# RWKV preparation of a hybrid encoder block: neighbour sums, norm sums, gate weights and one product taken from GpSimd or moved

## The chip, the cores and the metric

The kernel runs on one core of a Trainium2 chip. A core has a matrix engine (TensorE, "PE"; its weight loads are "PEld"), a vector engine (VectorE, "DVE"), a scalar engine for functions and copies (ScalarE, "ACT"), a general engine (GpSimd, "POOL") and an engine that issues transfers (SyncE, "SP"). Each works through its own queue in order; they wait for each other through semaphores. Data lies in SBUF (128 partitions) or, for the results of TensorE, in PSUM. The metric is the device time of one execution in microseconds (us), as the median of several runs.

## The reference, cut to what matters

One encoder layer on 1024 tokens of width 1024: a norm, one projection whose columns feed windowed attention, a bidirectional RWKV-7 branch and branch gates; then an output projection, a feed-forward part and a gated embedding. The preparation of the RWKV branch computes, for r, k and v (512 columns each):

```python
zr = proj[..., O_RWKV:O_GATE]
zr = zr + shift_mu[i] * (centred_shift(zr) - zr)      # 0.5 * (left neighbour + right neighbour)
...
w_raw = w0 + tanh(wl) @ w2                            # per direction, low rank 64
decay = exp(-exp(-softplus(-w_raw) - 0.5))
a = sigmoid(a0 + al @ a2)                             # per direction, low rank 64
kk = k * k_k
kk = kk / maximum(sqrt(sum(kk * kk, -1)), 1e-12)      # per head of 64
k_dir = k * (1.0 + (a - 1.0) * k_a)
...
bonus = sum(r * k_dir * r_k) * v                      # per head, both directions
...
gates = sigmoid(proj[..., O_GATE:].reshape(b, s, 2, D_MODEL))
```

The scan over the tokens then uses r, decay, k_dir, v, -kk and kk * a, and runs once forward and once backward.

## The kernel before

All matmuls with full precision are done as three: an operand is split into a rounded high part and a low part (the rest), and hi x hi, hi x lo and lo x hi are added in PSUM. `split` (L186) makes the two: a cast on ScalarE (L188) and a subtraction (L189) on VectorE or GpSimd, as the caller says. `load_w` (L194) loads a block of weights through a staging tile and splits it; its subtraction is on GpSimd unless `lo_eng` is given. Projection blocks give VectorE; the gates give none.

The stages follow each other: norm and q, k, v of the attention; the RWKV preparation (some 110 to 370 us of the profiled execution); attention; the chunked scan; the up projections, the output projection, the feed-forward part and the embedding. The program is written as a list of tiles and operations; a planner orders each engine's instructions at build time by its own costs and by the order of the program, except where the program pins them, and adds the waits. A tile with `bufs=n` has n buffers, and a new tile of that name waits until the oldest is free.

The preparation walks over four head pairs p (128 columns each). In order of the program, for one p:

- `keys` (L641): the k projection (48 matmuls of 512 columns, in two halves of the tokens), `shifted`, the squares of k * k_k (L644, ScalarE), their split for the norm sums.
- `normed_keys` (L649): the r projection by `proj_with`, which calls a hook after 36 of the 48 matmuls (`RH`): there the norm sums (`sums2`, L593 and L594: four matmuls with a matrix of ones) and a maximum with 1e-24 from PSUM (L655, VectorE). Behind the projection `shifted` for r, Ln and Exp (L658, L659, each with a table load on ScalarE) and the normed keys `kk` (L661).
- `direction(0)` (L667): the low-rank product for the decay (`lora`, four matmuls L569 and L571, Tanh from PSUM L573), scaled (L670) and summed along the chunks (L672); Exp of it both ways (`E`, `Ei`, L682 and L683); its last column kept (`Dt`, L684); -kk * E (L687, VectorE) and r * E (L688, GpSimd) into `ra`; the low-rank product for a; `kd` (L691, L692), `ta` (L693), the two halves of `bk` (L695, L696); r_k times kd (`rk`, L698, VectorE). `ra` and `bk` are stored by SP (L702, L703).
- the v projection with a hook after eight matmuls, which does the bonus sums of the pair before; `shifted` for v; the two low-rank products of the backward direction; `keys` of the next p; `direction(1)` (L700, L701 for rk); the bonus of this p begins; `normed_keys` of the next p.

`shifted` (L532) takes a projection from PSUM: ScalarE copies it once plainly into `zr`, which has a zero column on either side (L539), and once scaled by 1 - mu into `z` (L542). GpSimd adds the left and the right neighbour into `sm` (L544), and VectorE adds half of mu times it to `z` (L545). `zr` and `sm` have one buffer, `z` has four. The projections' PSUM tile `mm` has two banks, the others (`px`) six, the low-rank tile `th` two buffers.

The last pair has no next keys; gate projections (`gates`, L304) stand in for them. `fill0` (L618) takes a number of steps of them from `F0` at five points of the last pair. Each gate block has 24 matmuls, two weight loads of 256 KB, and a Tanh that goes out to HBM (L312, L313). What is left of them is done within the attention stage at the lowest priority.

Of the kernel before, what the change touches and what calls it, by code (L numbers as in the profile page):

```python
# [9 lines left out]
F32 = mybir.dt.float32  # L10
F32R = mybir.dt.float32r
AF = mybir.ActivationFunctionType
ALU = mybir.AluOpType
# [4 lines left out]
P = 128  # L18
T = 1024
DM = 1024  # L20
NT = T // P
KT = DM // P
C = 64
NCH = T // C
NP = 4
# [4 lines left out]
O_RWKV = 768  # L30
# [11 lines left out]
RH = 36  # L42
# [11 lines left out]
F0 = (28, 28, 28, 28, 40)  # L54
# [17 lines left out]
W_SCALE = -0.5 * float(np.exp(np.float64(-0.5)))  # L72
# [66 lines left out]
def block_kernel(ctx: ExitStack, tc: tile.TileContext, I: dict, out: bass.AP):  # L139
    nc = tc.nc  # L140
# [353 lines left out]
    def col(name, j):  # L494
        return pc[:, PC[name] + j:PC[name] + j + 1]


    with ExitStack() as s1:
# [15 lines left out]
        nc.vector.memset(wsc, W_SCALE)  # L514
        hka = A1.tile([P, 4], F32, name="hka")
# [16 lines left out]
        def shifted(c0, mi, pss=None, pin=False):  # L532
            pss = pss or proj(c0)
            zr = A1.tile([P, T + 2], F32, name="zr", bufs=1)
            nc.vector.memset(zr[:, 0:1], 0.0)
            nc.vector.memset(zr[:, T + 1:T + 2], 0.0)
            zc = z = A1.tile([P, T], F32, name="z", bufs=4)
            for h in range(2):
                a = nc.scalar.copy(zr[:, 1 + 512 * h:513 + 512 * h], pss[h])  # L539
                if pin and h == 0:  # L540
                    tc.keep_in_program_order(a)
                nc.scalar.activation(out=zc[:, 512 * h:512 * h + 512], in_=pss[h], func=AF.Copy, scale=omm[:, mi:mi + 1])  # L542
            sm = A1.tile([P, T], F32, name="sm", bufs=1)
            nc.gpsimd.tensor_tensor(out=sm, in0=zr[:, 0:T], in1=zr[:, 2:T + 2], op=ALU.add)  # L544
            a = nc.vector.scalar_tensor_tensor(out=z, in0=sm, scalar=hmu[:, mi:mi + 1], in1=zc, op0=ALU.mult, op1=ALU.add)  # L545
            if pin:
                tc.keep_in_program_order(a)
            return z
# [99 lines left out]

        def normed_keys(p, kz, sums):  # L649

            ri = nrm[:, 1]

            def norms():
                for hs, ps in next(sums):
                    nc.vector.tensor_scalar_max(ri[:, hs], ps, 1e-24)  # L655

            rz = shifted(O_RWKV + p * P, p, proj_with(O_RWKV + p * P, {RH: norms}))
            nc.scalar.activation(out=ri, in_=ri, func=AF.Ln)  # L658
            nc.scalar.activation(out=ri, in_=ri, func=AF.Exp, scale=-0.5)  # L659
            kk = A1.tile([P, T], F32, name="kk", bufs=1)  # L660
            nc.vector.scalar_tensor_tensor(out=kk, in0=kz, scalar=col("k_k", p), in1=ri, op0=ALU.mult, op1=ALU.mult)  # L661
            return kz, rz, kk

        def ch(x):
            return x.rearrange("p (c t) -> p c t", t=C)

        def direction(d, p, th, ta, kz, rz, kk, rk):  # L667

            th = th()
            nc.scalar.activation(out=th, in_=th, func=AF.Identity, scale=W_SCALE, bias=wsc)  # L670
            sl = slice(None) if d == 0 else slice(None, None, -1)
            nc.vector.tensor_tensor_scan(out=th[:, sl], data0=scan, data1=th[:, sl], initial=0.0, op0=ALU.mult, op1=ALU.add)  # L672
# [15 lines left out]
            nc.gpsimd.tensor_tensor(out=ra[:, :, 1, :], in0=ch(rz), in1=E2, op=ALU.mult)  # L688
            ta = ta()
# [7 lines left out]
            if d == 0:  # L697
                nc.vector.tensor_scalar_mul(rk, kd, col("r_k", p))  # L698
# [8 lines left out]
        for p in range(NP):  # L707
# [3 lines left out]
            def low_rank(d, i):  # L711
                th = lora(d, p, i, 8 * i + d * NP + p)
                fill0(p, 2 * d + i)
                return th
# [14 lines left out]
        fill0(NP - 1, 4)  # L729
# [1130 lines left out]
```

## Time and profile before

| what | us |
|---|---|
| median of 3 runs | 1809.24 |
| lowest and highest of them | 1803.22, 1815.18 |
| the profiled execution | 1803.17 |
| its span, first to last instruction | 1801.4 |
| TensorE busy | 1702.8 (95%) |
| VectorE, ScalarE, GpSimd busy | 1147.4 (64%), 882.0 (49%), 279.0 (15%) |

A row of the profile's groups or of its timeline gives line, engine, operation, the tile written and the tiles read, the shape, and times; in square brackets or at the end stands the idle time before the instruction and what ended it. In a group "x3 | 3.8, 1276 |" is the count, the busy time in us and the mean of one in ns. A list of waits gives the total in us, the number and the longest. Rows of stretches give the width and, for each engine, busy us and the number of instructions, then the granted TensorE clock (1 is full), the share of the DMA engines and GB/s. Matmuls are pipelined, so that their durations overlap: the distance of their starts counts.

### The profile page before, as it was taken

The page shows a single profiled execution, that of the slowest core. Times are in us where ns is not written, and L with a number is a line of the kernel's source. Part 1 is how long each engine was busy: PE and PEld are TensorE (multiplying, and loading weights), DVE is VectorE, ACT ScalarE, POOL GpSimd, SP SyncE. Part 2 cuts the span into 40 slices and gives each one's busy share as a digit, 9 for nine tenths or more (in the row PEclk, how much of TensorE's full clock was granted, in tenths as well). Part 3 has the DMA queues.
Part 4 walks back from the last instruction along what each step waited for, and adds up shares of the span by engine and source line. Part 5 has one row for each costly group of instructions (what it writes and reads, how often), then busy time and mean ns, then how long its engine had stood idle before and what let it go on. Part 6 is the DMA issues. An engine that isn't in the chain of part 4 may idle for free. (4 is left out here: it accounts for less than half of the span.)

```text
span 1801.4 us, 29643 instructions
## 1 busy us (share of the span) xinstructions
PE 1702.8 (95%) x11288; PEld 1367.5 (76%) x11288; DVE 1147.4 (64%) x1955; ACT 882.0 (49%) x1624; POOL 279.0 (15%) x241
## 2 busy tenths in 40 slices
PE   7999998899999898989889989999999999999998
PEld 7987675666677777867568867888888888888887
DVE  5667887345936556676564387767666877685432
ACT  5546775357754555456632255444444444554221
POOL 3343223331232121111232000000000000000000
PEclk9999999999999999999999999999999999999999
DMA  5353446574377474576565305454456983674111
GB/s 199 96 136 120 145 144 198 159 198 116 102 205 204 132 201 142 172 204 206 176 218 179 106 36 164 158 164 141 150 166 224 324 258 114 191 222 134 60 41 47
DMA packets 281998, 285.96 MB, mean 159 GB/s; under 512 B 49408, under 2 KB 195712, under 8 KB 281728
## 3 DMA queue, kind: packets, MB, share of 16 engines
q1 hardware_dynamic: 273600, 270.76, 48.9%
q0 software_dynamic: 7824, 12.59, 2.5%
q8 instruction: 89, 1.46, 0.3%
q10 hardware_dynamic: 432, 0.73, 0.1%
q14 instruction: 53, 0.43, 0.1%
HBM read 203.26 MB, written 80.74 MB: 158 GB/s over the span
## 5 line engine op out<-in xcount | busy, mean ns | idle before, releaser
L1742 PE MATMUL ff2ps<-th,sl 128*128 128x512 f32 x448 | 174.3, 389 | 0.0
L1742 PE MATMUL ff2ps<-tl,sh 128*128 128x512 f32 x448 | 174.3, 389 | 0.0
L1742 PE MATMUL ff2ps<-th,sh 128*128 128x512 f32 x448 | 173.9, 389 | 0.0
L189 POOL TENSOR_TENSOR wlo<-wst,whi 128x512 fp32r<-128x512 f32 x76 | 104.6, 1389 | 269.2 <-ACT whi L188 223.6
L176 POOL TENSOR_TENSOR rstd<-ms,neghalf 128x1 f32<-128x1 f32 x24 | 13.2, 552 | 791.3 <-DVE ms L174 791.3
L188 ACT CAST sh<-sst 128x512 fp32r<-128x512 f32 x109 | 67.7, 622 | 99.9 <-PE ff2ps L1742 51.3
L189 DVE TENSOR_TENSOR sl<-sst,sh 128x512 fp32r<-128x512 f32 x109 | 75.0, 688 | 47.5 <-ACT sh L188 47.3
L1742 PEld LDWEIGHTS ff2ps<-th,sh 128*128 128x128 f32 x448 | 84.0, 188 | 17.9 <-ACT th L188 0.3
L1742 PEld LDWEIGHTS ff2ps<-tl,sh 128*128 128x128 f32 x448 | 84.1, 188 | 17.6
L1742 PEld LDWEIGHTS ff2ps<-th,sl 128*128 128x128 f32 x448 | 84.1, 188 | 17.3
L188 ACT CAST whi<-wst 128x512 fp32r<-128x512 f32 x100 | 60.4, 617 | 60.8 <-DMA wst<-in_w_in_dram 22.9
L188 ACT CAST w1h<-w1st 128x512 fp32r<-128x512 f32 x48 | 28.4, 620 | 100.1 <-DMA w1st<-in_w_ff_dram 66.6
L189 DVE TENSOR_TENSOR w1l<-w1st,w1h 128x512 fp32r<-128x512 f32 x48 | 31.8, 687 | 54.5 <-ACT w1h L188 54.5
L209 PE MATMUL gps<-rm,bkp 128*128 128x256 f32 x256 | 62.4, 386 | 1.6 <-ACT tm L1105 0.9
L1078 DVE TENSOR_TENSOR gm<-gps,gmask 128x512 f32<-128x512 f32 x64 | 43.8, 688 | 29.6 <-PE gps L209 29.6
L219 PE MATMUL mm<-hh,wlo 128*128 128x512 f32 x144 | 58.4, 406 | 2.5 <-DVE wlo L189 2.5
L215 PE MATMUL gmm<-hh,whi 128*128 128x512 f32 x144 | 58.9, 409 | 1.6 <-ACT whi L188 1.4
L219 PE MATMUL gmm<-hh,wlo 128*128 128x512 f32 x144 | 59.3, 412 | 1.1 <-POOL wlo L189 1.1
L215 PE MATMUL mm<-hh,whi 128*128 128x512 f32 x144 | 58.6, 407 | 1.7 <-ACT whi L188 1.7
L217 PE MATMUL gmm<-hl,whi 128*128 128x512 f32 x144 | 58.7, 408 | 0.0
L217 PE MATMUL mm<-hl,whi 128*128 128x512 f32 x144 | 57.9, 402 | 0.0
L209 PEld LDWEIGHTS gps<-rm,bkp 128*128 128x128 f32 x256 | 47.2, 189 | 11.3 <-ACT tm L1105 2.1
(410 smaller groups left out, 4975.2 us busy)
## 6 DMA issues: line engine op xcount, KB each, us to landing
wst<-in_w_in_dram SPq DMA_DIRECT2D x92, 256.0 KB, 3.6
tst<-in_w_ff_dram SPq DMA_DIRECT2D x80, 256.0 KB, 3.9
w1st<-in_w_ff_dram SPq DMA_DIRECT2D x32, 512.0 KB, 5.4
hid_S<-h SPq DMA_DIRECT2D x64, 256.0 KB, 2.1
sst<-hid_S SPq DMA_DIRECT2D x64, 256.0 KB, 3.1
hid_A<-h SPq DMA_DIRECT2D x48, 256.0 KB, 2.0
sst<-hid_A SPq DMA_DIRECT2D x45, 256.0 KB, 3.5
ra_d<-ra SPq DMA_DIRECT2D x8, 1024.0 KB, 4.6
```

Of the source, the lines that this page charges most:

```text
L176: nc.gpsimd.tensor_tensor(out=r, in0=ms, in1=neghalf.broadcast_to([P, width]), op=ALU.pow)
L188: a = nc.scalar.copy(hi, src)
L189: b = (lo_eng or nc.vector).tensor_tensor(out=lo, in0=src, in1=hi.bitcast(F32), op=ALU.subtract)
L209: tc.keep_in_program_order(nc.tensor.matmul(*a, **kw))
L215: mm(ps, ah, bh, start=(i == 0), stop=False)
L217: mm(ps, ah, bl, start=False, stop=False)
L219: mm(ps, al, bh, start=False, stop=(i == n - 1))
L1078: nc.vector.tensor_tensor(out=gm[d][:, s % NB, 4 * h:4 * h + 4, :], in0=ps.rearrange("p j q t -> p (j q) t"), in1=gmask[:, d, :].unsqueeze ...
L1742: nc.tensor.matmul(banks[bs][i], x_[:, isl], y_, start=fresh and p + j == 0, stop=p == NPR - 1 and j == 2, skip_group_check=True)
```

## The change

- `shifted`: the copy into `zr` is scaled by half of mu; two additions on VectorE, of the left and then the right neighbour, go into `z`. `sm` and the GpSimd addition are gone; `zr` has two buffers.
- `normed_keys`: the decay's low-rank product of the forward direction, its scaling and its sum (`decays`) come ahead of the r projection, the product for a behind it, and the norm sums behind that, with no hook. The maximum becomes a Relu with a bias of -1e-24 on ScalarE, from PSUM, and Ln gets a bias of 1e-24.
- `direction`: r * E is on VectorE, the first `rk` on ScalarE; the low-rank tiles come from outside.
- the gates of the first seven blocks have their low parts made by VectorE; the filling steps of the last pair come at three points (56, 56, 40) rather than five (28, 28, 28, 28, 40).

```diff
-RH = 36
...
-F0 = (28, 28, 28, 28, 40)
+F0 = (56, 56, 40)
...
-    def gates(h, ms=range(2 * KT), mm=nc.tensor.matmul):
+    def gates(h, ms=range(2 * KT), mm=nc.tensor.matmul, lo_of=lambda m: nc.gpsimd):
...
-            hi, lo = load_w(PW, "w", w_in[:, :, c0:c0 + P], P, parts=2)
+            hi, lo = load_w(PW, "w", w_in[:, :, c0:c0 + P], P, parts=2, lo_eng=lo_of(m))
...
+        tiny = A1.tile([P, 2], F32, name="tiny")
+        nc.vector.memset(tiny[:, 0:1], -1e-24)
+        nc.vector.memset(tiny[:, 1:2], 1e-24)
...
-            zr = A1.tile([P, T + 2], F32, name="zr", bufs=1)
+            zr = A1.tile([P, T + 2], F32, name="zr", bufs=2)
...
-            zc = z = A1.tile([P, T], F32, name="z", bufs=4)
+            z = A1.tile([P, T], F32, name="z", bufs=4)
             for h in range(2):
-                a = nc.scalar.copy(zr[:, 1 + 512 * h:513 + 512 * h], pss[h])
...
-                nc.scalar.activation(out=zc[:, 512 * h:512 * h + 512], in_=pss[h], func=AF.Copy, scale=omm[:, mi:mi + 1])
-            sm = A1.tile([P, T], F32, name="sm", bufs=1)
-            nc.gpsimd.tensor_tensor(out=sm, in0=zr[:, 0:T], in1=zr[:, 2:T + 2], op=ALU.add)
-            a = nc.vector.scalar_tensor_tensor(out=z, in0=sm, scalar=hmu[:, mi:mi + 1], in1=zc, op0=ALU.mult, op1=ALU.add)
...
+                nc.scalar.activation(out=zr[:, 1 + 512 * h:513 + 512 * h], in_=pss[h], func=AF.Copy, scale=hmu[:, mi:mi + 1])
+                nc.scalar.activation(out=z[:, 512 * h:512 * h + 512], in_=pss[h], func=AF.Copy, scale=omm[:, mi:mi + 1])
+            for i in (0, 2):
+                nc.vector.tensor_tensor(out=z, in0=z, in1=zr[:, i:i + T], op=ALU.add)
             return z
...
-        gates0 = gates(0)
+        gates0 = gates(0, lo_of=lambda m: nc.vector if 25 * m < sum(F0) else nc.gpsimd)
...
+        def low_rank(p, d, i):
+            return lora(d, p, i, 8 * i + d * NP + p)
+
         def normed_keys(p, kz, sums):
 
             ri = nrm[:, 1]
-
-            def norms():
-                for hs, ps in next(sums):
-                    nc.vector.tensor_scalar_max(ri[:, hs], ps, 1e-24)
-
-            rz = shifted(O_RWKV + p * P, p, proj_with(O_RWKV + p * P, {RH: norms}))
-            nc.scalar.activation(out=ri, in_=ri, func=AF.Ln)
+            th = decays(0, low_rank(p, 0, 0))
+            rz = shifted(O_RWKV + p * P, p)
+            ta = low_rank(p, 0, 1)
+
+            for hs, ps in next(sums):
+                nc.scalar.activation(out=ri[:, hs], in_=ps, func=AF.Relu, bias=tiny[:, 0:1])
+            nc.scalar.activation(out=ri, in_=ri, func=AF.Ln, bias=tiny[:, 1:2])
             nc.scalar.activation(out=ri, in_=ri, func=AF.Exp, scale=-0.5)
...
-            return kz, rz, kk
+            return th, ta, kz, rz, kk
...
+        def decays(d, th):
+
+            nc.scalar.activation(out=th, in_=th, func=AF.Identity, scale=W_SCALE, bias=wsc)
+            sl = along(d)
+            nc.vector.tensor_tensor_scan(out=th[:, sl], data0=scan, data1=th[:, sl], initial=0.0, op0=ALU.mult, op1=ALU.add)
+            return th
+
         def direction(d, p, th, ta, kz, rz, kk, rk):
...
-            nc.gpsimd.tensor_tensor(out=ra[:, :, 1, :], in0=ch(rz), in1=E2, op=ALU.mult)
-            ta = ta()
+            nc.vector.tensor_tensor(out=ra[:, :, 1, :], in0=ch(rz), in1=E2, op=ALU.mult)
...
             if d == 0:
-                nc.vector.tensor_scalar_mul(rk, kd, col("r_k", p))
+                nc.scalar.activation(out=rk, in_=kd, func=AF.Copy, scale=col("r_k", p))
...
+            fill0(p, 0)
             rk = A1.tile([P, T], F32, name="rk", bufs=1)
-            direction(0, p, lambda: low_rank(0, 0), lambda: low_rank(0, 1), *ops, rk)
+            direction(0, p, *ops, rk)
             vz = shifted(O_RWKV + 1024 + p * P, 8 + p, proj_with(O_RWKV + 1024 + p * P, {VH: lambda: bonus and next(bonus)}))
-            lows_ = [low_rank(1, i) for i in range(2)]
+            th, ta = (low_rank(p, 1, i) for i in range(2))
+            fill0(p, 1)
             nxt = keys(p + 1) if p + 1 < NP else None
-            direction(1, p, lambda: lows_[0], lambda: lows_[1], *ops, rk)
+            direction(1, p, decays(1, th), ta, *ops[2:], rk)
...
-        fill0(NP - 1, 4)
+        fill0(NP - 1, 2)
```

More of the change, by code (lines that the diff above doesn't have):

```diff
@@ L530, in block_kernel, with shifted @@
         nc.sync.dma_start(scan, I["scan"])
[L532 removed]
+        def shifted(c0, mi, pss=None):
             pss = pss or proj(c0)
[L534 removed]
+            zr = A1.tile([P, T + 2], F32, name="zr", bufs=2)
             nc.vector.memset(zr[:, 0:1], 0.0)
             nc.vector.memset(zr[:, T + 1:T + 2], 0.0)
[L537 removed]
+            z = A1.tile([P, T], F32, name="z", bufs=4)
             for h in range(2):
[L539 to L547 removed]
+                nc.scalar.activation(out=zr[:, 1 + 512 * h:513 + 512 * h], in_=pss[h], func=AF.Copy, scale=hmu[:, mi:mi + 1])
+                nc.scalar.activation(out=z[:, 512 * h:512 * h + 512], in_=pss[h], func=AF.Copy, scale=omm[:, mi:mi + 1])
+            for i in (0, 2):
+                nc.vector.tensor_tensor(out=z, in0=z, in1=zr[:, i:i + T], op=ALU.add)
             return z
@@ L661, in normed_keys, with along @@
             nc.vector.scalar_tensor_tensor(out=kk, in0=kz, scalar=col("k_k", p), in1=ri, op0=ALU.mult, op1=ALU.mult)
-            return kz, rz, kk
+            return th, ta, kz, rz, kk
         def ch(x):
             return x.rearrange("p (c t) -> p c t", t=C)
+        def along(d):
+            return slice(None) if d == 0 else slice(None, None, -1)
+        def decays(d, th):
[3 more added lines that the diff above has]
+            return th
         def direction(d, p, th, ta, kz, rz, kk, rk):
[L669 to L672, printed above, removed]
+            sl = along(d)
             Lc = ch(th)
```

4 lines of the change are left out of this document (removed).

## The prediction

> **What bounds the kernel now.** I read the page first: one core, and TensorE all but full.
>
> ```profile
> span 1801.4 us, 29643 instructions
> PE 1702.8 (95%) x11288; PEld 1367.5 (76%) x11288; DVE 1147.4 (64%) x1955; ACT 882.0 (49%) x1624; POOL 279.0 (15%) x241
> ```
>
> The profiled execution took 1803.17 us, 1.8 more than its span. With PE at 95%, a change that leaves every matmul in place can pay only by the time in which PE waits, and by the slow matmuls after a wait. So the second view is the waits of PE inside the preparation and what follows it (110 to 400 us); the columns are the total, the number and the longest.
>
> ```profile
> PE px L593 <- ACT s L188: 11.1, 3, 4.6
> PE px L594 <- DVE s2l L189: 2.8, 1, 2.8
> PE mm L219 <- DVE wlo L189: 2.5, 2, 1.4
> ...
> PE mm L215 <- ACT whi L188: 1.7, 1, 1.7
> PE gmm L215 <- ACT whi L188: 1.4, 1, 1.4
> PE gmm L219 <- POOL wlo L189: 1.1, 2, 0.6
> ```
>
> These are 20.6 us. More than half is one place, met three times: the norm sums (L593), which stand inside the r projection after 36 of its 48 matmuls and want the hi part `s` of the squared keys. The first head pair has no such wait. The third view is PE in order of time. Each pair of rows is the first matmul after a wait and the first at full pace again; three pairs are norm sums, the fourth the bonus sums of the last pair.
>
> ```profile
> 186.25 0.80 PE L593 MATMUL px<-s,one_r 128*128 128x512 f32 x1 [4.04 <-ACT s L188]
> 189.60 0.40 PE L219 MATMUL mm<-hh,wlo 128*128 128x512 f32 x1
> ...
> 231.82 0.49 PE L593 MATMUL px<-s,one_r 128*128 128x512 f32 x1 [2.46 <-ACT s L188]
> 237.37 0.63 PE L569 MATMUL px<-lr,wlrh 128*128 128x512 f32 x2
> ...
> 280.10 0.80 PE L593 MATMUL px<-s,one_r 128*128 128x512 f32 x1 [4.57 <-ACT s L188]
> 285.17 0.39 PE L215 MATMUL mm<-hh,whi 128*128 128x512 f32 x1
> ...
> 353.95 0.79 PE L594 MATMUL px<-s2l,one_r 128*128 128x512 f32 x1 [2.77 <-DVE s2l L189]
> 360.08 0.43 PE L215 MATMUL gmm<-hh,whi 128*128 128x512 f32 x1
> ```
>
> Between 280.10 and 285.17 stand 11 matmuls, 0.46 us apart, where the pace elsewhere is 0.23: 5.07 - 11 x 0.23 = 2.5 us lost on top of the wait. By the same count the others lose 1.7 (7 matmuls), 2.1 (14, with a second wait of 0.23) and 2.9 (14). A norm wait thus costs 5.8, 4.8 and 7.1 us: **17.7 in all**.
>
> The Trainium skill ("TensorE: Matmul & The Clock Gate", Part 1) says that the clock halves after an idle window of about 3.4 us. By that rule the waits of 2.46 and 2.77 us would be followed by no slow stretch, and the sum below would be 2.1 lower; here both were, so the rows decide.
>
> Why is `s` late? The fourth view is the stretch before the wait at 231.82.
>
> ```profile
> 222.13 1.99 POOL L544 TENSOR_TENSOR sm<-zr 128x1024 f32<-128x1024 f32 x1 [0.93 <-POOL ra L688]
> 222.29 2.91 DVE L695 SCALAR_TENSOR_TENSOR bk<-th,Ei 128x1024 f32<-128x1024 f32 x1
> 228.66 1.27 DVE L545 SCALAR_TENSOR_TENSOR z<-sm,hmu,z 128x1024 f32<-128x1024 f32 x1
> 229.97 1.15 ACT L644 ACTIVATE nrm<-z,pc 128x1024 f32<-128x1024 f32 x1 [7.38 <-DVE z L545]
> ```
>
> POOL has the neighbour sum at 224.12, VectorE adds it only at 228.66, behind the backward direction's products, and ScalarE stands 7.38 us for it. VectorE is what is late, and it is slowed by POOL:
>
> ```profile
> 202.00 0.17 DVE L684 COPY Dt<-E 128x16 f32<-128x16 f32 x1
> 202.09 3.25 DVE L687 SCALAR_TENSOR_TENSOR ra<-kk,E 128x1024 f32<-128x1024 f32 x1
> ...
> 207.53 1.21 DVE L695 SCALAR_TENSOR_TENSOR bk<-th,Ei 128x1024 f32<-128x1024 f32 x1
> 208.67 2.38 DVE L698 TENSOR_SCALAR rk<-kd,pc 128x1024 f32<-128x1024 f32 x1
> ...
> 219.07 2.17 DVE L684 COPY Dt<-E 128x16 f32<-128x16 f32 x1
> 221.15 1.21 DVE L687 SCALAR_TENSOR_TENSOR ra<-kk,E 128x1024 f32<-128x1024 f32 x1
> ```
>
> ```profile
> 218.10 3.10 POOL L688 TENSOR_TENSOR ra<-z,E 128x1024 f32<-128x1024 f32 x1 [7.61 <-ACT E L682]
> ```
>
> ```profile
> 165.59 0.74 DVE L698 TENSOR_SCALAR rk<-kd,pc 128x1024 f32<-128x1024 f32 x1
> ```
>
> The same copy takes 0.17 alone and 2.17 beside POOL's 218.10 to 221.20; likewise 3.25 against 1.21, 2.38 against 0.74, 2.91 against 1.21. One cycle (one head pair) loses 2.00 + 2.04 + 1.64 + 1.70 = 7.4 us so.
>
> **The change part by part.** One cycle, from norm sums to norm sums, and the stretch after the last of them, with the busy time of PE, its weight loads, VectorE, ScalarE and POOL:
>
> ```profile
> 186.25:231.82 45.57, 43.11 (x176) 32.66 (x177) 40.21 (x44) 31.48 (x45) 11.31 (x5) 0.96 0.49 147
> ...
> 280.10:373.05 92.95, 82.25 (x321) 61.00 (x321) 45.82 (x38) 43.39 (x66) 39.85 (x29) 0.94 0.60 183
> ```
>
> PE's share without its wait and its slow stretch is 45.57 - 2.46 - 1.7 = 41.4; VectorE is busy 40.2, ScalarE 31.5. The prices:
>
> ```profile
> L672 DVE TENSOR_TENSOR_SCAN th<-scan,th 128x1024 f32<-128x1024 f32 x2 | 4.6, 2286 | 1.2 <-ACT th L670 1.2
> ...
> L655 DVE TENSOR_SCALAR nrm<-px 128x512 f32<-128x512 f32 x2 | 1.4, 691 | 0.5 <-PE px L594 0.5
> ```
>
> ```profile
> L573 ACT ACTIVATE th<-px,hb 128x512 f32<-128x512 f32 x8 | 4.9, 693 | 0.0
> ...
> L691 ACT ACTIVATE kd<-th,oka,hka 128x1024 f32<-128x1024 f32 x2 | 2.5, 1274 | 0.0
> ```
>
> *Neighbour sums as two additions, three times a cycle.* An addition of a tile with a copy of itself shifted by one element is not in the trace. From below 0.74 (the one-input form of that size), from above 3.25; I take 1.21, the two-input rows alone. So 2 x 1.21 - 1.27 (the row of 228.66) = +1.15 each, +3.4. POOL's part goes. *r by E on VectorE*: two of 1.21, +2.4. *Maximum to ScalarE as Relu*: -1.4 on VectorE; on ScalarE 2 x 0.69 as L573, which also reads PSUM with a bias. Bounds nothing (hidden in ScalarE's free time) and 1.27 (L691, twice the size); 0.69 because L573 has the same shape and form. *First rk to ScalarE*: -0.74, +1.27 as L691. *Scaled copies for plain ones*: six, each at no more than L573's 0.69; I count 0.1 more for each, +0.6. *Locks gone*: -7.4.
> VectorE: 40.2 + 3.4 + 2.4 - 1.4 - 0.7 - 7.4 = **36.5**; ScalarE 31.5 + 1.4 + 1.3 + 0.6 = **34.8**. Both lie under PE's 41.4, and PE becomes the bound of the cycle.
>
> *Norm sums moved behind the low-rank products.* They pass the last 12 matmuls of r (12 x 0.23 = 2.8) and two low-rank products:
>
> ```profile
> 147.06 0.73 PE L569 MATMUL px<-lr,wlrh 128*128 128x512 f32 x2
> ...
> 148.38 0.50 PE L215 MATMUL mm<-hh,whi 128*128 128x512 f32 x1
> ```
>
> 1.3 us for one product. PE asks for the sums 2.8 + 2.6 = 5.4 us later, and each of the three waits (4.04, 2.69, 4.57) is shorter than that. They would be gone if `s` came no earlier. Will it come later? At worst the moved first scan (2.3), the second addition (1.15) and one new r by E (1.21) all go ahead of it, 4.7; in that stretch the locks give back 2.00 + 1.70, so `s` is 1.0 late against a spare of 1.4, 2.7 and 0.8. At best the key's additions no longer wait for POOL and run 5 us sooner. The moved low-rank product issues no DMA; the weights two projections ahead are asked for where they were, on SP. Relu, Ln and Exp wait for the later sums on ScalarE, and behind them stand the copies that free the PSUM banks for v: that is the wait the change adds (a rival). The second low-rank tile has two buffers, and its Tanh can wait for the last bk.
> I take the 17.7 whole.
>
> *After the last norm sums* the gate projections fill PE. By the list of PE's waits they are 1.1 for POOL's wlo, 1.7 and 1.4 for ScalarE's whi, 2.5 for VectorE's wlo, and the 2.8 with 2.9 of slow matmuls: 12.4 in all.
>
> ```profile
> 308.03 0.69 ACT L573 ACTIVATE th<-px,hb 128x512 f32<-128x512 f32 x1 [3.01 <-DVE bk L695]
> 308.62 0.61 ACT L188 CAST whi<-wst 128x512 fp32r<-128x512 f32 x1
> ```
>
> ScalarE's cast for v's weights stood behind a Tanh that waited for VectorE's bk, so the 1.7, and the 2.5 with it, stem from VectorE's products of that stretch. With the locks gone I count both: -4.2, from nothing (POOL's gate parts held VectorE too, and seven of them now run on it) to that. The 2.8 comes from a scratch tile that the gates use too, the 1.4 from a weight load; I leave them.
> *Low parts of seven gates on VectorE*: 14 instructions of 0.68 instead of POOL's 1.47.
>
> ```profile
> L189 POOL TENSOR_TENSOR wlo<-wst,whi 128x512 fp32r<-128x512 f32 x36 | 52.5, 1470 | 89.5 <-ACT whi L188 89.5
> L189 DVE TENSOR_TENSOR wlo<-wst,whi 128x512 fp32r<-128x512 f32 x24 | 15.7, 683 | 9.5 <-ACT whi L188 9.5
> ```
>
> That is 9.5 us on an engine that was busy 46 of these 93; but in its queue they stand behind products of 1.21 each, and behind each stands SP's next weight load, which waits for its staging tile. From -2.5 (the 1.1 and the 1.4 go) to +39 (the slower rival below); I take +1.7, one more wait like the largest one here. The blocks of 56 gate steps put four to five weight loads ahead of the first direction's stores; the stores are read only in the next stage.
>
> **Sum:** 17.7 + 4.2 - 1.7 = 20.2 us less, 1803.2 to 1783.0 for the profiled execution. The median of the three runs shown is 1809.24, 6 above that execution (they lie from 1803.22 to 1815.18), so **1789.0**. Gates not done here are done in the attention stage; PE's work is only moved.
>
> **The rivals.** *All waits go*, the bonus wait too: 17.7 + 12.4, 1779. For it: POOL idle, VectorE 5 us a cycle below PE. Against: the 2.8 is not POOL's.
> *The wait moves*: ScalarE keeps its order, and v's first matmul waits for a PSUM bank behind Square, Relu and Ln. For it: ScalarE stood 7.38 us before Square with ready copies behind. Against: the Square no longer waits for POOL. Half of the 17.7 stays: 1797; all of it: 1806.
> *The change doesn't do what it says*: the long VectorE instructions are long for another reason than POOL. VectorE is then 43.9 a cycle, above PE's 41.4: three cycles of 2.5 are lost, and the 4.2 too: 20.2 - 11.7 = 8.5 less, 1801. Against: all four coincide with a POOL instruction. The Trainium skill ("SBUF — State Buffer", Who interferes with whom) says that POOL and VectorE share a pair of SBUF ports, which one instruction holds to its end while the other stands still; by that rule this rival could not be, and the four rows agree with it.
> *Slower*: the gates' low parts wait in VectorE's queue, the two weight buffers run dry and every gate starves PE once, at the row of 353.95 (2.8 + 2.9 = 5.7 us). From four starved gates on the gain is gone; all seven are 39 against 17.7 (I leave the other terms out): 1831.
>
> **How the numbers follow.** Forecast 0.50 (1781 to 1796), all waits go 0.13, the wait moves 0.21, not POOL 0.09, slower 0.07. The range 1778 to 1806 leaves out the slower case, part of the first rival and a little of the others. About 1% (18 us) is what a measurement of this kernel tells from no change; 1791 lies inside the forecast, three quarters of it below: 0.38 + 0.13 for faster by more, 0.42 within, 0.07 slower.
>
> **What would show it.** No L593 wait in PE's list, and full clock in the three cycles; cycles of 41 to 42 us; Dt copies all at 0.17; two additions of 1.21 a tile; VectorE near 36.5 a cycle; no POOL instruction before the gates of the attention stage. I am wrong if a v matmul waits for ScalarE's z, if an addition takes over 2 us, if a gate waits for `wlo` of VectorE, or if the attention stage, now with more gates, shows new waits of PE.

## The result, and the profile after

The changed kernel takes 1789.59 us (median, 1787.7 to 1792.1) against 1810.57 (1803.22 to 1815.18) for the kernel before in the same set of runs: a ratio of **0.9889** (95% interval 0.9853 to 0.9925). Timed again later beside other kernels it took 1787.85 (0.9894, 0.9875 to 0.9912). One run of a kernel below, `r * E` alone, took 5132.65 us and stands apart from its other five: it is counted in that kernel's median of 1797.16 (1796.41 without it) and not in its ratio.

The page's first lines: PE is as full as it was, VectorE has 13.5 us less to do in spite of 26 more instructions, POOL 74 us less.

```profile
span 1787.4 us, 29590 instructions
PE 1696.6 (95%) x11288; PEld 1368.4 (77%) x11288; DVE 1133.9 (63%) x1981; ACT 893.8 (50%) x1636; POOL 205.0 (11%) x205
```

PE's waits from 110 to 290 us, the three cycles and the first gates, in the view of waits (total, number, longest):

```profile
PE gmm L218 <- DVE wlo L188: 0.7, 1, 0.7
PE gmm L214 <- ACT whi L187: 0.3, 1, 0.3
```

Of the 11.1 us for the norm sums nothing is left. The norm sums of the second and the fourth pair, in order of time:

```profile
188.20 0.50 PE L590 MATMUL px<-s,one_r 128*128 128x512 f32 x1
...
270.68 0.50 PE L590 MATMUL px<-s,one_r 128*128 128x512 f32 x1
```

From one to the other 82.48 us pass, where it was 280.10 - 186.25 = 93.85. The two cycles between, each with the busy time of PE, its weight loads, VectorE, ScalarE and POOL, the granted clock, the DMA share and GB/s, and the stretch from there to the first score:

```profile
188.20:229.44 41.24, 41.24 (x178) 31.77 (x177) 36.60 (x46) 34.68 (x49) 0.00 (x0) 1.00 0.57 166
229.44:270.68 41.24, 41.24 (x177) 31.75 (x176) 35.91 (x45) 33.85 (x48) 0.00 (x0) 1.00 0.56 163
270.68:354.91 84.23, 72.80 (x303) 56.45 (x303) 39.43 (x45) 40.06 (x61) 13.43 (x13) 0.96 0.68 205
```

PE has no gap in the cycles and the full clock; POOL does nothing. VectorE's groups from 100 to 290 us (busy time, mean ns, idle time before):

```profile
L544 DVE TENSOR_TENSOR z<-z,zr 128x1024 f32<-128x1024 f32 x26 | 31.8, 1223 | 2.0 <-ACT z L542 1.6
...
L695 DVE TENSOR_TENSOR ra<-z,E 128x1024 f32<-128x1024 f32 x7 | 8.6, 1223 | 0.1
...
L691 DVE COPY Dt<-E 128x16 f32<-128x16 f32 x7 | 1.1, 162 | 0.8 <-ACT E L689 0.8
```

An addition takes 1.22 us, r * E 1.22, and every Dt copy 0.16: no long row is left.

The last stretch has a new wait, the longest of the preparation:

```profile
294.08 0.79 PE L214 MATMUL gmm<-hh,whi 128*128 128x512 f32 x1 [6.53 <-ACT gth L311]
...
298.87 0.39 PE L214 MATMUL mm<-hh,whi 128*128 128x512 f32 x1
```

From 294.08 to 298.87 stand 11 matmuls, so 4.79 - 11 x 0.23 = 2.3 us are lost behind the wait: 8.8 in one place. What ScalarE did before it:

```profile
291.35 0.62 ACT L187 CAST whi<-wst 128x512 fp32r<-128x512 f32 x1 [9.13 <-DMA wst<-in_w_in_dram]
291.88 1.15 ACT L704 ACTIVATE rk<-kd,pc 128x1024 f32<-128x1024 f32 x1
292.93 0.60 ACT L187 CAST whi<-wst 128x512 fp32r<-128x512 f32 x1
293.44 1.07 ACT L311 ACTIVATE gth<-gmm 128x512 f32<-128x512 f32 x2
```

The gate's Tanh `gth`, which empties the PSUM bank, stands in ScalarE's queue behind a cast of weights that had been 9.13 us without its load, and behind the `rk` that the change gave to ScalarE and one more cast. And the loads from 279 to 294 us (KB each, median us from issue to landing):

```profile
kT<-kT_d POOLq DMA_DIRECT2D x1, 2048.0 KB, 8.3
ra_d<-ra SPq DMA_DIRECT2D x1, 1024.0 KB, 11.4
wst<-in_w_in_dram SPq DMA_DIRECT2D x3, 256.0 KB, 9.3
```

The 2 MB of kT, the 1 MB of `ra` and the gates' weights are under way at once; a weight block of 256 KB needs 9.3 us. In the kernel before, loads from 262 to 300 us, a block took 4.4 in the median. There kT goes out only at 291.48, 9.8 us later than with the change, and the next weight blocks are asked for when it has almost landed, at 298.85:

```profile
kT<-kT_d POOLq DMA_DIRECT2D x1, 2048.0 KB, 8.0
...
wst<-in_w_in_dram SPq DMA_DIRECT2D x4, 256.0 KB, 4.4
```

Then the attention stage, from the first score to the first state sums:

```profile
354.91 0.71 PE L886 MATMUL sc<-kT,qT 128*128 128x256 f32 x4 [2.69 <-DMA qT<-qT_d]
...
530.14 1.15 PE L208 MATMUL sps<-UV,tm 128*64 128x64 f32 x32
```

It begins 18.1 us earlier than before (373.05) and lasts 175.2 us; before, its last row was

```profile
543.35 1.15 PE L209 MATMUL sps<-UV,tm 128*64 128x64 f32 x32
```

that is 170.3. From there to the end of the span it is 1257.3 against 1258.1. So the two profiled executions differ by 18.1 - 4.9 + 0.8 = 14.0 us.

### The profile page after: what moved, and what is told of

Same layout as the page of the kernel before. It is cut to its first block, busy times and chain, and to the rows that moved or that the text cites. A ratio compares the mean times of both kernels' runs of the same rounds, so it can differ in the third digit from the quotient of the medians.

```text
span 1787.4 us, 29590 instructions
## 1 busy us (share of the span) xinstructions
PE 1696.6 (95%) x11288; PEld 1368.4 (77%) x11288; DVE 1133.9 (63%) x1981; ACT 893.8 (50%) x1636; POOL 205.0 (11%) x205
## 5 line engine op out<-in xcount | busy, mean ns | idle before, releaser
L188 POOL TENSOR_TENSOR wlo<-wst,whi 128x512 fp32r<-128x512 f32 x62 | 80.9, 1318 | 299.1 <-ACT whi L187 228.2
L1745 PEld LDWEIGHTS ff2ps<-tl,sh 128*128 128x128 f32 x448 | 84.1, 188 | 17.7
L1133 DVE COPY Wt<-wps 64x512 f32<-64x512 f32 x16 | 10.9, 680 | 70.3 <-PE wps L208 70.3
L796 DVE TENSOR_TENSOR tmp<-Lp,Z 128x31 f32<-128x31 f32 (+15 forms) x124 | 52.8, 426 | 2.9 <-POOL Z L791 0.5
L188 DVE TENSOR_TENSOR w1l<-ssum,w1h 128x512 fp32r<-128x512 f32 x64 | 43.0, 687 | 16.2 <-ACT w1h L187 16.2
```

The lines of the kernel that those rows point to most:

```text
L188: b = (lo_eng or nc.vector).tensor_tensor(out=lo, in0=src, in1=hi.bitcast(F32), op=ALU.subtract)
L796: nc.vector.tensor_tensor(out=tv, in0=Lp[:, t + 1:32, t:t + 1].broadcast_to([P, n, m]), in1=Z[:, t:t + 1, 0:m].broadcast_to([P, n, m]), op ...
L1745: nc.tensor.matmul(banks[bs][i], x_[:, isl], y_, start=fresh and p + j == 0, stop=p == NPR - 1 and j == 2, skip_group_check=True)
```

## Experiments

All times are medians in us; ratios are to the kernel before, run on the same chip. "Two cycles" is the time from the first matmul of the second norm sums to that of the fourth, "last" from there to the first score, "attention" from there to the first state sums, "rest" from there to the end of the span, each from the one profiled execution. The same kernel twice gives 1263.0 and 1259.4 for the rest, and 1257.3 and 1257.5; so a few us there tell nothing. Where the sums stand in the middle of r ("old place"), "last" holds 5.4 us more work, 12 matmuls of r and two low-rank products ("in r": 4.1, one product less; "at 44": 3.5, eight matmuls less).

| kernel | time | ratio (95%) | place | two cycles | last | attention | rest |
|---|---|---|---|---|---|---|---|
| before | 1807.6 to 1810.6 | 1 | old | 93.9 | 93.0 | 170.3 | 1258.1 |
| changed | 1789.59 | 0.9889 (0.9853 to 0.9925) | new | 82.5 | 84.2 | 175.2 | 1257.3 |
| changed, again | 1787.85 | 0.9894 (0.9875 to 0.9912) | new | 82.5 | 83.5 | 175.8 | 1257.5 |
| order alone | 1793.71 | 0.9906 (0.9881 to 0.993) | new | 86.4 | 87.0 | 169.2 | 1263.9 |
| engines alone | 1783.25 | 0.9851 (0.9828 to 0.9875) | old | 85.3 | 81.0 | 170.4 | 1263.0 |
| engines alone, again | 1781.59 | 0.986 (0.9841 to 0.988) | old | 85.1 | 82.0 | 170.3 | 1259.4 |
| changed, GpSimd sums | 1789.02 | 0.9888 (0.9865 to 0.991) | new | 84.6 | 84.9 | 169.9 | 1260.0 |
| changed, kT later | 1784.72 | 0.986 (0.9833 to 0.9887) | new | 82.5 | 82.2 | 172.2 | 1255.0 |
| changed, gate lows on GpSimd | 1790.16 | 0.9897 (0.986 to 0.9934) | new | 82.5 | 82.6 | 170.9 | 1267.3 |
| changed, sums in the hook | 1787.25 | 0.9881 (0.9832 to 0.993) | in r | 83.9 | 86.9 | 174.8 | 1262.2 |
| engines, kT later | 1783.29 | 0.9868 (0.9825 to 0.9911) | old | 84.7 | 85.4 | 170.8 | 1266.7 |
| engines, GpSimd sums | 1791.74 | 0.9904 (0.9876 to 0.9933) | old | 85.7 | 85.6 | 170.2 | 1259.9 |
| r * E alone | 1797.16 | 0.9933 (0.9909 to 0.9957) | old | 87.7 | 90.9 | 172.1 | 1261.9 |
| engines, sums at 44 | 1788.33 | 0.9896 (0.988 to 0.9913) | at 44 | 88.0 | 82.2 | 170.2 | 1261.6 |

**Order alone**: the changed kernel with the old engines, so the order of the change and nothing else.

```
-  nc.scalar.activation(out=zr[...], ..., scale=hmu[...]); for i in (0, 2): nc.vector.tensor_tensor(z, z, zr[:, i:i + T], add)
+  nc.scalar.copy(zr[...], pss[h]); nc.gpsimd.tensor_tensor(sm, zr[:, 0:T], zr[:, 2:T + 2], add); nc.vector.scalar_tensor_tensor(...)
-  Relu on ScalarE; rk on ScalarE; r * E on VectorE; lo_of=...
+  maximum on VectorE; rk on VectorE; r * E on GpSimd; gates' low parts on GpSimd
```

> The order of the change alone (norm sums behind the low-rank products, the first scan ahead of r, the gates' steps at three points); neighbour sums, r by E and the gates' low parts stay on GpSimd, maximum and rk on VectorE. Theory A (the place of the sums and VectorE's relief each do part): each of the three waits was shorter than the 5.4 us by which the sums are asked for later, so the L593 waits fall from 11.1 us to 0 to 2, VectorE still shows Dt copies of 2.2 us beside GpSimd, cycles of 41 to 43 us instead of 45.6 and 48.3; 8 to 16 us faster than before, ratio 0.991 to 0.996. Rival B (VectorE is the bound of the cycle, and the place only moves the wait): the waits stand at the sums or at the next projection again, cycles of 45 us or more, ratio 0.997 to 1.003.

**Engines alone**: the kernel before, its norm sums at 36, its low-rank products and its five gate pieces, with the engines of the change.

> The engines of the change alone (no GpSimd arithmetic, maximum and first rk on ScalarE, low parts of seven gates on VectorE); the norm sums stay in the r projection after 36 matmuls, the low-rank products where they were. Theory A: VectorE gets to k's additions some 5 us sooner, which is more than the waits of 4.0, 2.7 and 4.6; the L593 waits fall from 11.1 to 0 to 3 us in all, no Dt copy over 0.2 us, VectorE near 36.5 us a cycle; 8 to 17 us faster than before, ratio 0.990 to 0.996. Rival B (the place decides, VectorE's relief does not reach PE): the L593 waits stay at 8 us or more, ratio 0.996 to 1.002.

Order alone gives 1793.71, engines alone 1783.25: either takes most of the gain, the two don't add up, and **the engines alone beat the whole change** (confirmed on one chip below). They also beat theory A of their own text, which had 8 to 17 us: by the traces they win 4.4 ahead of the second norm sums, 8.6 in the two cycles and 11.9 in the last stretch, for which the prediction had 6.7 (4.2 of waits and 2.5 of slow matmuls). PE's waits with the engines alone, 110 to 400 us:

```profile
PE gmm L215 <- ACT gth L312: 2.8, 1, 2.8
...
PE px L591 <- ACT s L188: 1.4, 1, 1.4
```

At its old place the norm sum waits once, 1.4 us, where it was 11.1 in three: with VectorE relieved, `s` comes in time. With the order alone no norm sum waits at all (the bonus sums behind them do, four times 0.2 to 0.7 in the cycles), but PE waits 5.7 us for ScalarE's `vt` in the last stretch, and the cycles are 3.9 longer than in the change. Its Dt copies take 456 ns in the mean instead of 1507 (100 to 290 us): the new order by itself takes most of them out of GpSimd's way, where I had expected them to stay at 2.2 us.

**GpSimd sums** and **kT later**, both on the changed kernel. The first puts the neighbour sums back on GpSimd with one VectorE operation behind them (as in the fence above); the second holds the load of kT until v of the last pair is written:

```
-  if p == NP - 2: kT = PY.tile(...); nc.gpsimd.dma_start(kT, kT_d)
+  if p == NP - 1:                                  # behind vz = shifted(...)
+      kT = PY.tile(...); nc.gpsimd.tensor_copy(kT[:, 0, 0, 0:1], vz[:, 0:1]); nc.gpsimd.dma_start(kT, kT_d)
```

> The changed kernel with only the neighbour sums back on GpSimd (one GpSimd addition and one VectorE instruction in place of two VectorE additions). Theory A: VectorE does 3.4 us a cycle less work of its own and loses 3 to 5 us to GpSimd's instructions, so its cycle stays below PE's 41 us; as PE is the bound, the time is that of the changed kernel within 4 us, ratio to before 0.987 to 0.992. Rival C (the neighbour sums on GpSimd were what made PE wait): the L593 waits are back with 5 us or more, ratio 0.993 to 0.999.

> The changed kernel with the 2 MB load of the attention's keys (kT) held until v of the last pair is there, some 35 us later. In the changed kernel PE waits 6.5 us at 294 for a gate Tanh that stands behind a weight cast on ScalarE, which waits 9.1 us for its weights while kT is loaded; 2.5 us of slow matmuls follow. Theory K (kT's load takes the DMA engines from the gate weights): that wait is gone or under 1.5 us, weights land in under 5 us there, 5 to 9 us faster than the changed kernel, ratio to before 0.984 to 0.987. Rival Q (SP issues the weights late behind its own waits for VectorE's low parts): the wait at that place stays at 4 us or more and the time is that of the changed kernel, 0.987 to 0.991.

The GpSimd sums make no difference to the time in this order (1789.02), but the stages differ both ways: the first score comes 2.0 to 4.1 us later than in the two traces of the change (356.88 against 354.91 and 352.81), and attention is 5.3 to 5.9 shorter. The later kT is 4.3 below that kernel on the same chip and 4.9 below the first time of the change, a little less than theory K's 5 to 9, and its trace shows the cause of the new wait. The two weight blocks that the change asks for right behind kT (loads from 280.5 to 281.6 us), and PE's waits for gate tiles from 110 to 400:

```profile
wst<-in_w_in_dram SPq DMA_DIRECT2D x2, 256.0 KB, 3.2
```

```profile
PE gmm L214 <- ACT whi L187: 3.6, 3, 2.0
...
PE mm L214 <- ACT z L542: 2.0, 1, 2.0
...
PE gmm L214 <- ACT gth L311: 0.3, 1, 0.3
```

They land after 3.2 us instead of 9.4, although the store of `ra` still follows them (282.49), and the 6.5 us for `gth` are 0.3. Most of it comes back as smaller waits (2.0 for `z`, 3.6 for `whi`, where the load is now): "last" falls by 2.0 only.

**Gate lows on GpSimd**, the changed kernel with one edit undone (`gates0 = gates(0)`):

> The changed kernel with one edit undone: the low parts of the first gate column blocks go back to GpSimd (1.27 us each there, 0.59 us on VectorE in the rows seen so far). Theory T1, by the term of the prediction: VectorE's share of the lows is worth 1.7 us in the last stretch, so about 1791 against 1789.6. Theory T2: the last stretch hangs on the 256 KB weight loads, which these lows only follow, so nothing: 1789 to 1790, and the longest wait there is still for a gate tile behind a weight load. Theory T3: VectorE issues its other work sooner without the lows, so 1787 or less.

1790.16, but the interval, 1784 to 1798 in time, holds all three theories, and my 1.7 us can't be told from nothing. The trace doesn't fit T2: the wait of 6.5 us for `gth` isn't there (the longest is 2.7, for `vt`). Here only one weight block is asked for right behind kT (283.76), and it lands after 4.7 us. Attention is 170.9, and the 7.3 us won until then are lost behind it (rest 1267.3). Whether that loss belongs to this kernel or to this execution stays open.

**Engines alone with kT later**, the same edit on the better kernel:

> The kernel before with only the engines of the change (norm sums in the middle of r's products, gates in five pieces), and in addition the 2 MB load of kT held back until v of the last pair is written, as in the run of the changed kernel with that edit. Theory K (kT shares the DMA engines with the gate weights and holds them up): the wait of 2.77 us for a gate tile at 290 us and the 0.91 clock behind it go, so 1779 to 1781 against 1783.3 without the later load. Rival K0 (kT was clear of the weights in this order, being 3.6 us earlier than in the changed kernel): 1783. Rival K-: the later load meets the last gate weights and the last writes of ra and bk, and waits of 2 us twice come up there, so 1785 to 1787.

1783.29: K0 by the time. By the trace K's wait, the 2.77 us for `gth` at 290, is gone (1.1 for a later `gth` is left, at 325.62), but a wait of 3.0 for `s2h` of the bonus came (the profiled execution was the slowest of its four, 1791.75). So kT is in the weights' way in this order too; it costs less here.

**Sums in the hook**, the changed kernel with the norm sums at the old place:

```
-  rz = shifted(O_RWKV + p * P, p)
-  ta = low_rank(p, 0, 1)
-  for hs, ps in next(sums): Relu
+  rz = shifted(O_RWKV + p * P, p, proj_with(O_RWKV + p * P, {36: norms}))     # norms: the sums and Relu
+  ta = low_rank(p, 0, 1)
```

> The changed kernel with the norm sums put back inside r's products (after product 36 of 48), everything else as changed: the low-rank products of direction 0 stay ahead and behind r. Theory E (with VectorE relieved and GpSimd silent the sums are ready in time wherever they stand; their late place only delays kk, and with it the release of the buffer that kT is loaded into): kT starts 3 to 5 us earlier than 281.66, the wait of 6.53 us falls below 4, and the time is 1785 to 1787. Theory S, that of the prediction (the later place is what saves the three waits): waits of 2 to 4 us come back at three sums with their slow stretches, 1797 to 1803. Theory 0: neither, 1789 to 1790.

This is against my prediction's reason. The only wait that comes back at a norm sum is one of 0.65 us, and 1787.25 is no slower than the change. The interval is wide (its four times lie from 1779.65 to 1794.68), so between E and 0 it doesn't decide; S is out. kT started at 280.37, no earlier than in the change's second trace (280.30), and the longest gate wait is 3.7.

**Engines alone with GpSimd sums**, all but the two additions:

> The kernel before with the engines of the change except for the neighbour sums, which stay one GpSimd addition and one VectorE operation behind it (the norm sums in the middle of r's products, gates in five pieces). Theory N: in this order it is the GpSimd addition in the key's path (2.1 us and its hand-overs, and the VectorE copy of 2.17 us beside it) that makes the norm sums late, so waits of 2 to 3 us at three sums stay, 1790 to 1796. Theory M: the other moves (maximum, r*E, r_k off their engines) free VectorE enough alone: 1783 to 1786, as the same edit made no difference in the changed kernel's order. Theory W: nothing is left of the gain without the two additions, 1803 to 1809.

1791.74: theory N by the time, but only in part by its sign. VectorE stands for POOL's sum, which itself is stretched while VectorE works:

```profile
176.13 4.17 POOL L545 TENSOR_TENSOR sm<-zr 128x1024 f32<-128x1024 f32 x1 [11.39 <-ACT zr L542]
```

```profile
180.34 1.28 DVE L546 SCALAR_TENSOR_TENSOR z<-sm,hmu,z 128x1024 f32<-128x1024 f32 x1 [1.78 <-POOL sm L545]
```

Two of its norm sums wait, 1.02 and 1.25 us, where theory N had 2 to 3 at all three, and the two cycles are only 0.4 to 0.6 longer than with the engines alone. More is lost in the last stretch (85.6 against 81.0 and 82.0), where PE waits 3.7 us for `whi`. So in the old order the additions are worth 8 to 10 us by the times (1783.25 and 1781.59 against it, on other chips), and that they are worth it at the norm sums is not shown; in the new order nothing is left in the total.

**r * E alone**: the kernel before with one word changed (`nc.gpsimd` to `nc.vector` in L688).

> The kernel before with one line changed: r*E (ra's second half) on VectorE instead of GpSimd, nothing else. Theory R, from the rows of the kernel before and of the engines without the additions: it is r*E of 2.7 us on GpSimd, ahead of the key's neighbour sum there and beside VectorE's copy of Dt (2.17 us against 0.17), that makes the norm sums late; then the copies take 0.17 us, the three waits fall to 1 to 2 us, and the time is 1792 to 1798 against 1809.5 before. Rival D (VectorE's own load makes them late, and 1.2 us of r*E twice a pair adds to it): the waits stay at 2.5 to 4.5, 1806 to 1812.

```profile
L684 DVE COPY Dt<-E 128x16 f32<-128x16 f32 x7 | 1.2, 175 | 1.2 <-ACT E L682 1.1
L684 DVE COPY Dt<-E 128x16 f32<-128x16 f32 x6 | 9.0, 1507 | 0.0
```

The first row is of this kernel, the second of the kernel before, both in 100 to 290 us: the same copies take 175 ns instead of 1507. `ra`, next in VectorE's queue, takes 1221 instead of 1889, and the first `rk` 741 instead of 1833. GpSimd's neighbour sums stay, and other rows now meet them: the first half of `bk` takes 2248 instead of 1961, the scan 2521 instead of 2286. Two norm sums wait, 0.83 and 2.59 us, instead of three. The time is 12 us lower by the ratio (0.67%), theory R. More instructions on VectorE, and VectorE is done sooner: it is busy 38.3 and 40.1 us in the two cycles instead of 40.2 and 41.1. That `r * E` also stands ahead of the keys' sum in GpSimd's queue is not the reason: in the kernel before, those sums were ready at 178.2, 224.1 and 272.4 us, and VectorE took each of them 4.5 us later. One line of the change holds more than half of what the change brings.

**Engines alone again**, **sums at 44** and **the change again**, on one chip with the last one:

> The same kernel as in the run of the engines alone, timed beside the changed kernel on one chip, since the two were 1783.3 and 1789.6 in different calls. Theory O (the new order costs some us in the last stretch, where kT's load meets the gate weights): 5 to 7 us below the changed kernel, 1782 to 1785. Rival N (the difference lay between chips): within 2 us of it.

> The changed kernel itself, unedited, timed beside the engines alone on one chip: 1788 to 1791 by its first runs. Its second trace shows which of the waits of the first come back: by theory K the one of 6.5 us for a gate tile at 294 us does, and the attention stage's 4.9 us more than before do not if they were a chance of that one execution (the kernel with GpSimd sums in the same order had 169.9 us there, the kernel before 170.3).

> The engines alone with the norm sums after product 44 of 46 of r instead of 36. Theory: the one wait of 1.37 us left at a norm sum, with its slow stretch of 1 to 2 us, goes, and the stretch of the cycles comes nearer to that of the changed kernel (93.2 against 96.3 us in the traces), so 1780 to 1782. Rival: kk comes 2 us later, kT's load and r's side with it, and eats it up: 1783 to 1785.

Engines alone 1781.59, the change 1787.85: 6.3 us apart again, so theory O has the size. Its place is only partly that of O. The wait of 6.5 did come back, in the same place:

```profile
292.65 0.80 PE L214 MATMUL gmm<-hh,whi 128*128 128x512 f32 x1 [6.46 <-ACT gth L311]
```

but so did the long attention stage, 175.8 us, which I had held for a possible chance. From the traces of the two kernels on this chip: the new order wins 2.6 in the two cycles, and 1.1 ahead of them, loses 1.5 + 5.4 = 6.9 in the last stretch, 5.5 in attention, and has 1.8 less behind it; together 6.8, the difference of the spans (1786.1 and 1779.3). The second of the two losses is in a stage that the change doesn't touch. The program text of that stage is the same in both kernels; the order in which PE's instructions are written out is not. Among these kernels there are three such orders: the change, its repeat and the later kT share one (172.2 to 175.8 us); the kernel before, the change with GpSimd sums, the one with sums in the hook and r * E alone share the second (169.9 to 174.8); all the others the third (169.2 to 170.9), which is close to the second. In the change's order, PE waits at one place for VectorE:

```profile
442.30 2.15 PE L907 MATMUL pt<-ident,smk 128*128 128x128 f32 x9 [2.60 <-DVE smk L904]
```

```profile
438.49 2.91 DVE L896 TENSOR_TENSOR es<-es,sums 128x4 f32<-128x4 f32 x1
```

```profile
438.87 2.50 POOL L188 TENSOR_TENSOR wlo<-wst,whi 128x512 fp32r<-128x512 f32 x2
```

A VectorE instruction on 4 elements a partition takes 2.91 us: it is the lock again, beside two gate parts on POOL (438.87 to 441.37). The repeat and the later kT have it in the same place, the engines alone have no such row; the columns are the number, and the shortest, median and longest of the 16 in ns:

```profile
L896 DVE TENSOR_TENSOR es<-es,sums x16: 149/160/2910, 358.1 to 477.3; 128x4 f32<-128x4 f32 x16
```

```profile
L891 DVE TENSOR_TENSOR es<-es,sums x16: 151/162/164, 355.0 to 471.1; 128x4 f32<-128x4 f32 x16
```

The lock is only a part of the loss. PE's waits for `smk` in this stage are 3.4 us with the change, 1.8 in the kernel before; all its waits behind the first score are 10.8 against 7.2. And the order alone doesn't set the length: the later kT has the first order and the same wait of 2.6, and 172.2; the sums in the hook have the second order, no such wait, and 174.8. The granted clock is 0.97 in the three stages of 174.8 us and more, 0.98 to 1.00 in the others. Why the order of attention comes out differently, and what the rest of the loss is, was not tried.

The sums at 44 (of 48) were a miss: 1788.33, 6.7 above the same kernel with 36. No norm sum waits, as expected, but `kk` comes later, ScalarE does `E`, `Ei` and `rk` of the forward direction later, and v's copies out of PSUM stand in its queue behind them:

```profile
201.95 1.14 ACT L696 ACTIVATE rk<-kd,pc 128x1024 f32<-128x1024 f32 x1
...
205.08 0.68 ACT L543 ACTIVATE z<-mm,omm 128x512 f32<-128x512 f32 x1
```

So the first matmul of the next k projection waits for a PSUM bank in all three cycles:

```profile
PE mm L227 <- ACT z L543: 2.6, 3, 1.1
```

That is 2.6 us; the clock is 0.91 in two windows of 20 us around the second and the third of them (190 to 210, 250 to 270), 1.00 around the first (150 to 170). Neither theory had this time. The late `kk` is the rival's, but what it costs in the cycles, 2.9 us, is a cousin of "the wait moves" of the prediction: ScalarE's order, and a PSUM bank that is emptied late. Another 2.2 of the 7.7 us between the two spans lie behind attention, where a few us tell nothing.

## Why the prediction was right, and where it was not

**The time** came out where I put it, in part by luck: two misses have opposite signs. The sum was 20.2 us less than the profiled execution; the traces show 18.1 less at the first score, and 14.0 at the end. I then added 6 for the distance between the profiled execution of before and the median, and the changed kernel has no such distance (its profiled execution 1789.22, its median 1789.59). By the medians the gain is 21.0 us, and 19.8 in the repeat, close to the sum; by the stages of the traces, on which the sum was built, it is less.

**The cycle** was right, in its sums and in the prices that decide them. VectorE 36.5: measured 36.60 and 35.91. ScalarE 34.8: 34.68 and 33.85. PE 41.4 as the bound: 41.24. Additions 1.21: 1.22. Dt copies 0.17: 0.16. The part of the 17.7 us that lies between the second and the fourth norm sums is the first slow stretch, the second wait with its own, and the third wait: 1.7 + 2.69 + 2.1 + 4.57 = 11.1; measured 93.85 - 82.48 = 11.4.

**The reason for the 17.7** was too narrow. I had put it on the sums' new place, with the freed VectorE as a help that only had to make `s` not later. The runs show that either is enough for the larger part: at the old place the waits are gone too once VectorE is free (0.65 and 1.4 us are left), and with the old engines the new place does it. *Not POOL* is out: r * E alone makes the long rows short.

**The last stretch** was mis-sized. I counted 4.2 for waits that go, less 1.7 for the low parts. Taking the 5.4 us of moved work and the slow stretch of 2.5 out of the 92.95, 85.1 are left, against 84.2: 0.8 less instead of 2.5. The old waits are gone, as I said; what I left out is shown by the issues of kT, the first row of the change, the second of the engines alone:

```profile
281.66 0.56 POOL L730 DMA_DIRECT2D kT<-kT_d  x1 [163.11 <-DVE kk L661]
```

```profile
278.09 0.56 POOL L725 DMA_DIRECT2D kT<-kT_d  x1 [161.33 <-DVE kk L659]
```

kT goes into the buffer that the norms leave when `kk` is done, and with the sums moved, `kk` is later. Right behind kT two gate weight blocks are asked for in both kernels. The first row is again of the change (loads from 281.8 to 282.8 us), the second of the engines alone (279.3 to 280.4):

```profile
wst<-in_w_in_dram SPq DMA_DIRECT2D x2, 256.0 KB, 9.4
```

```profile
wst<-in_w_in_dram SPq DMA_DIRECT2D x2, 256.0 KB, 7.6
```

In both they land 0.8 to 2.2 us after kT does (289.92 and 286.27), so a later kT makes them later: 291.33 and 292.16 with the change, 287.06 and 287.83 with the engines alone, where PE's wait for `gth` is 2.8 and not 6.5. The store of `ra`, 2.1 us behind kT in the change and 7.9 with the engines alone, matters less: with the GpSimd sums in the old order it is 7.5 behind, and the two blocks took 8.7. Where no block is asked for right behind kT, as with `r * E` alone (kT at 281.36, blocks from 288.71 after 3.5 and 3.7), no gate waits for `gth`. I counted queues for the moved steps and not the buffer that they hold. The low parts cost one wait of 0.7 us that can be seen, for `wlo` of VectorE (282.02; one of the signs that I had named), and not 1.7; the slower rival had no other sign for it.

**Attention** was named among what would make me wrong, and valued at nothing. It took 4.9 us, the largest miss: PE's instructions have a different order in the same stage, and in it stands the very lock that I had costed in the preparation, for some 1.6 us of waits. The rest of the 4.9 stays open.

The Trainium skill's rule ("SBUF — State Buffer", Who interferes with whom), that GpSimd and VectorE share a pair of SBUF ports of which one instruction at a time holds the lock, agrees with the runs: 1507 against 175 ns for the Dt copies, 2.91 us against a median of 0.16 for the small instruction in attention. Its clock rule, an idle window of about 3.4 us ("TensorE: Matmul & The Clock Gate", Part 1), does not fit the slow stretch behind a wait of 0.73 us that is shown at the end; here the measurement decides.

## What to carry to other kernels

Before pricing a GpSimd instruction by its own duration, look at what VectorE does beside it: r * E, 2.7 us there, moved to VectorE, where it costs 1.2, freed more time than it took, and alone it was worth over half of what the change brought. When a step is moved, follow the tiles it keeps alive as well as the queues it passes: here a buffer that came free 1.7 to 3.6 us later held up the 2 MB load into it, and with that load the gate weights that were asked for right behind it. And try each half of a change alone: two cures for one wait don't add, and one of them can carry a cost of its own.

## What was not expected of the hardware

- A POOL addition that takes 1.9 us elsewhere in the same trace took 4.17 beside VectorE's products (the row at 176.13; VectorE was busy until 178.6): the stretching goes both ways.
- PE's clock can fall behind short waits too. With the sums at 44, PE had a wait of 0.73 us behind the low-rank products (granted clock 1.00 in 203 to 206 us); the eight matmuls behind it stood 0.43 us apart for 3.4 us, at a granted clock of 0.57 in 206 to 210:

```profile
205.81 0.65 PE L227 MATMUL mm<-hh,whi 128*128 128x512 f32 x1 [0.73 <-ACT z L543]
206.26 0.63 PE L228 MATMUL mm<-hl,whi 128*128 128x512 f32 x1
...
209.56 0.39 PE L227 MATMUL mm<-hh,whi 128*128 128x512 f32 x1
```

```profile
203.00:206.00 3.00, 2.27 (x7) 1.00 0.47 131
206.00:210.00 4.00, 4.00 (x11) 0.57 0.95 285
```

Not every wait does this: one of 1.10 us at 163.35 in the same trace was followed by a clock of 1.00 (150 to 170).

- The executions of one kernel differ with the mean granted clock: ten executions of the kernel before on one chip went from 1801.39 us at 0.984 to 1818.62 at 0.975. Which stretch makes the difference was not looked at; a single profiled execution is a sample of this spread, and the 6 us of my offset lay in it.
